# A two-layer encoder step on one core: TensorE kept in program order within the gate and up products, and the norm's roots placed between them

## The chip, the core and the metric

The kernel runs on one core of a Trainium2 chip. A core has TensorE for matrix products (PE in the profile; its weight loads are listed apart as PEld), VectorE (DVE), ScalarE (ACT), GpSimd (POOL) and SyncE (SP), which issues most transfers. Each takes its own queue of instructions in order and waits on semaphores for the others. The metric is the device time of one execution in microseconds; less is better.

## The reference

One step of a hybrid streaming encoder for 560 columns: 512 frames of a new stream, 32 frames of a running stream and 16 meta tokens, each a vector of 1024. Two layers; each is a feed-forward half-step, a mixer, and another feed-forward half-step. The first layer's mixer is a gated linear attention (GLA), the second's a latent attention (MLA).

```python
def rmsnorm(x, w):
    x32 = x.astype(jnp.float32)
    y = x32 * lax.rsqrt(jnp.mean(x32 * x32, axis=-1, keepdims=True) + RMS_EPS)
    return (y * w.astype(jnp.float32)).astype(x.dtype)

def swiglu_half(h, norm_w, w_gate, w_up, w_down):
    hn = rmsnorm(h, norm_w)
    return h + 0.5 * ((jax.nn.silu(hn @ w_gate) * (hn @ w_up)) @ w_down)

for i in range(DEPTH):
    hp = swiglu_half(hp, ffn1_norm[i], ffn1_w_gate[i], ffn1_w_up[i], ffn1_w_down[i])
    ...
    xp = rmsnorm(hp, mix_norm[i])
    ...                       # GLA for i = 0, MLA for i = 1; hp = hp + dp
    hp = swiglu_half(hp, ffn2_norm[i], ffn2_w_gate[i], ffn2_w_up[i], ffn2_w_down[i])
```

All data is float32. The inner size of the feed-forward part is 2816, that is 22 tiles of 128.

## The kernel before

**Layout.** Activations lie with the 1024 features on partitions, as 8 tiles of 128, and the columns beside each other. The state `h` stays on the chip. The columns are treated in two halves of 280 (272 in the last feed-forward part, which leaves the meta tokens out). Each float32 operand is split into a rounded high part and the rest: ScalarE casts the high part (`whi`, `ah`, `x`; L323), VectorE subtracts to get the low part (`wlo`, `al`, `x`; L324). A product is then high x high, low weight x high, high weight x low: lines 352, 353 and 355 in `mm`, where 352 and 353 alternate over the tiles of the sum, so that the second matmul of a product already needs `wlo`.

**Four feed-forward parts.** `ffn` goes over groups of the 22 inner tiles, and in a group over pairs of tiles. `gate_up` makes gate and up for a pair with seven products instead of eight, by a Strassen-like scheme over a 2 x 2 split of the input (4 feature tiles by half of the columns). The products are called by their operand and are written in this order: b11 into bank pair A, b21 into C, t6 added into A, t5 into B, t7 added into A, t4 into C, b22 added into B. Each is 24 matmuls. `quads` loads the four weight quarters (tile `fr`, L429), adds them on VectorE (L438), and hands out the split weights one product at a time; three of its additions stand ahead of the weight of t6. After a product, `copy` (L483) or `finish` (L489 to L499) takes results out on ScalarE and VectorE; `finish` multiplies by the norm's root `yn`, applies silu and splits the result into `ah` and `al`. Between two products `gap` lets `ffn` put in pieces of the product down of the group before (tile `Y`, bank pair of its own, result added into `h` on L544). The last group's down is written after all pairs of the part.

**The operands of a feed-forward part** are made while `h` gets its last additions, tile by tile: class `Quads` writes for each feature tile the split operand, the combinations t5, t6, t7, t4 of it, and the square of `h`, summed over tiles in `acc`. In the first part (`lazy`) there is no earlier product, so that each operand and the squares are made when first asked for.

**The norm's roots.** The operands carry the norm's weight but not the root of the mean square, which is one number per column; it is multiplied in at the end, by `finish`. `roots` makes it short: three matmuls with one column each sum `acc` over partitions and put 280 sums into three columns (L394, six instructions each time), VectorE does the root on a 128 x 3 tile (L408 to L416, eleven small operations one after the other), and the returned function transposes the three columns against the identity (L401), which gives the root in every partition; `scale` copies it to `yn` on ScalarE (L264). `rsqrt_mean` makes it long: one sum with all columns (L380), and the same root on a 128 x 280 tile with squares on ScalarE (L412). `scale` of class `Normed`, which the two mixers use, is long; `scale` of `Quads` is short, and makes sums, root and transposes at one place, the first `finish`.

**The order** of instructions on each engine is not the written order. The library plans it: it runs the program in a simulation and gives an engine the first written instruction among those that are ready there. So the written order is a priority, and what the simulation believes to be late falls behind.

Of the kernel before, what the change touches and what calls it, by code (L numbers as in the profile page):

```python
# [10 lines left out]
F32 = mybir.dt.float32  # L11
# [7 lines left out]
P = 128  # L19
D = 1024  # L20
ND = D // P
# [31 lines left out]
def weight_plan():  # L53
# [3 lines left out]
    def ffn(i, l):  # L57
        for gi, (f0, f1) in enumerate(GROUPS):
# [3 lines left out]
            for m in range(ND):  # L62
                plan.append((("d", i, l, gi, m), f1 - f0))

    ffn(1, 0)
    for h in range(GH):
        plan.extend((("v", h, j), nk * V_COLS[h] / P) for j, nk in enumerate(V_PARTS[h]))
# [4 lines left out]
        if h >= 2:  # L72
            plan.extend((("go", h - 2, c), 8) for c in range(4))
    ffn(2, 0)
    ffn(1, 1)
    for m in range(6):
        plan.append((("wd", m), 8))
# [18 lines left out]
class Normed(list):  # L96
# [3 lines left out]
    def __init__(self, net, name, halves):  # L100
        self.net, self.w0, self.halves, self.y = net, NORM_COLS[name], halves, None
        self.squared, self.scaled = [0, 0], [False, False]
# [22 lines left out]
    def scale(self, hf):  # L125
        c = slice(*self.halves[hf])
        if not self.scaled[hf]:
            while self.squared[hf] < ND:
                self.square(hf)
            self.net.rsqrt_mean(hf, self.y[:, c], c.stop - c.start, D)  # L130
            self.scaled[hf] = True
        return self.y[:, c]


class Quads(Normed):
# [10 lines left out]
    def __init__(self, net, name, halves, pool, tmp):  # L146
        super().__init__(net, name, halves)
        self.pool, self.tmp = pool, tmp
        self.n = halves[0][1]
        self.sets, self.kept, self.made = None, {}, set()  # L150
        self.lazy, self.early = False, []

    def place(self, op, i):

# [74 lines left out]
    def make(self, op):  # L229
# [24 lines left out]
                net.split(*self.place("b22", i), b22)  # L254
        self.made.add(op)

    def scale(self, hf):
        net = self.net
        c0, c1 = self.halves[hf]
        if not self.scaled[hf]:  # L260
            if self.lazy:
                for m in range(ND):
                    Normed.square(self, hf)
            net.nc.scalar.copy(self.y[:, c0:c1], net.roots(hf, c1 - c0, D)())  # L264
            self.scaled[hf] = True
        return self.y[:, c0:c1]

# [14 lines left out]
class Net:  # L282
# [90 lines left out]
            nc.scalar.activation(sq[:, :n], src, AF.Square)  # L373
            nc.vector.tensor_tensor(acc[:, :n], acc[:, :n], sq[:, :n], op=ALU.add)

    def rsqrt_mean(self, half, y, n, dim):

        nc = self.nc
        s = self.bank("s")
        nc.tensor.matmul(s[:, :n], self.ones, self.accs[half][:, :n], start=True, stop=True)  # L380
        vh = self.np_.tile([P, 280], F32, name="vh", tag="vh", bufs=1)
        t = self.np_.tile([P, 280], F32, name="t", tag="t", bufs=1)
        self.rsqrt(y, s[:, :n], vh[:, :n], t[:, :n], dim)

    def roots(self, half, n, dim):

        pe = self.nc.tensor
        acc = self.accs[half]  # L390
        s = self.bank("s")
        first = (0, P, n - P)
        for j, c in enumerate(first):
            pe.matmul(s[:, j:j + 1], acc[:, c:c + P], self.ones[:, :1], start=True, stop=True)  # L394
        y, vh, t = (self.np_.tile([P, 3], F32, name=x, tag=x) for x in ("ry", "rv", "rt"))
        self.rsqrt(y, s[:, :3], vh, t, dim)

        def finish():
            out = self.bank("s")
            for j in (2, 0, 1):  # L400
                pe.transpose(out[:, first[j]:first[j] + P], y[:, j:j + 1].to_broadcast([P, P]), self.ident)  # L401
            return out[:, :n]

        return finish
# [55 lines left out]
    def gate_up(self, i, l, f, xs, act, raws, tp, between):  # L460


        nc = self.nc
        v = nc.vector
        n = xs.n
        left = self.quads(i, l, f, raws, xs.early)
        done = []

        def product(to, op, more=False):
            if xs.lazy and op in ("b11", "b21"):  # L470
                w, x = next(left), xs.operand(op)
            else:
                x, w = xs.operand(op), next(left)
            for j in range(2):
                self.mm(to[:, j, :n], w, 4 * j, x, (0, n), more)

        def gap():
            done.append(0)
            between(len(done))

        def copy(of, tag):
            r = tp.tile([P, 2, 280], F32, name="r", tag=tag, bufs=1)
            nc.scalar.copy(r[:, :, :n], of[:, :, :n])  # L483
            return r

        def finish(j, hf, bank, r, how):
            gu = tp.tile([P, 2, 280], F32, name="gu", tag="gu", bufs=2)
            b, r, t = bank[:, :, :n], r[:, :, :n], gu[:, :, :n]
            if how == "neg":  # L489
                v.scalar_tensor_tensor(t, b, -1.0, r, op0=ALU.mult, op1=ALU.subtract)  # L490
            else:
                v.tensor_tensor(t, b, r, op=how)
            y = xs.scale(hf).unsqueeze(1).to_broadcast([P, 2, n])
            v.tensor_tensor(t, t, y, op=ALU.mult)
            g, u = gu[:, 0, :n], gu[:, 1, :n]
            nc.scalar.activation(g, g, AF.Silu)
            v.tensor_tensor(g, g, u, op=ALU.mult)
            c = slice(*xs.halves[hf])
            self.split(act[j][0][:, c], act[j][1][:, c], g)  # L499

        A = self.bank2("A")
        product(A, "b11")
        r1 = copy(A, "ra")
        gap()
        C = self.bank2("C")
        product(C, "b21")
        first = xs.lazy and "t6" not in xs.made
        if not first:
            finish(0, 0, C, r1, ALU.add)
        gap()  # L510
        product(A, "t6", True)
        r2 = copy(A, "rb")
        gap()
        B = self.bank2("B")
        product(B, "t5")
        p5 = copy(B, "rc")
        if first:
            finish(0, 0, C, r1, ALU.add)
        gap()
        product(A, "t7", True)  # L520
        r3 = copy(A, "ra")
        finish(1, 1, A, p5, "neg")
        gap()
        D = self.bank2("C")
        product(D, "t4")
        finish(1, 0, D, r3, ALU.subtract)
        gap()
        product(B, "b22", True)
        finish(0, 1, B, r2, ALU.add)
        gap()  # L530
# [19 lines left out]
    def ffn(self, i, l, xs, halves, side, turn):  # L550


        ap, fw = Pools(self.tc, side), Pools(self.tc, side)
        acp = ap(f"act{i}{l}")
        if xs.lazy:
            free = [acp.tile([P, 2, T // 2], F32, name="xt", tag=f"a{x}{j}") for j in range(4, 8) for x in "hl"]
            xs.tmp = [t[:, k, :] for t in free for k in range(2)]
        raws, tp = fw(f"raw{i}{l}", 6), fw(f"tmp{i}{l}", 1)
        fill = []
        last = len(GROUPS) - 1  # L560
        for gi, (f0, f1) in enumerate(GROUPS):
            j0 = 4 * (gi % 2) if gi < last else 0
            acts = [(acp.tile([P, T], F32R, name=f"ah{j}", tag=f"ah{j}"),
                     acp.tile([P, T], F32R, name=f"al{j}", tag=f"al{j}")) for j in range(j0, j0 + 4 if gi == last else j0 + f1 - f0)]
            slots = [7 * min((f1 - f0) // 2, 2) - 1]

            def between(k):
                if slots[0] <= 0 or (slots[0] == 7 * min((f1 - f0) // 2, 2) - 1 and k < 2):
                    return
                for _ in range(-(-len(fill) // slots[0])):  # L570
                    fill.pop(0)()
                slots[0] -= 1

            for f in range(f0, f1, 2):
                if gi == last and f == f0 + 4:
                    assert not fill
                    acts += [(acp.tile([P, T], F32R, name=f"ah{j}", tag=f"ah{j}"),
                              acp.tile([P, T], F32R, name=f"al{j}", tag=f"al{j}")) for j in range(4, 8)]
                self.gate_up(i, l, f, xs, acts[f - f0:f - f0 + 2], raws, tp, between)
            assert not fill  # L580
            order = [(m, hf) for m in range(ND) for hf in (0, 1)]
            if gi < last:
                fill = self.down(i, l, gi, acts, halves, order)
        fw.close()
        after = turn()
        order = Quads.ORDER if isinstance(after, Quads) else (
            [(0, 0), (1, 0), (0, 1), (1, 1), (2, 0), (3, 0), (2, 1), (3, 1)] + [(m, hf) for hf in (0, 1) for m in range(4, 8)])
        for f in self.down(i, l, last, acts, halves, order, after):
            f()
        ap.close()  # L590
# [966 lines left out]
```

## Time and profile before

| | us |
|---|---|
| median of 3 runs | 2114.17 |
| lowest, highest | 2113.81, 2117.72 |
| the profiled execution | 2115.19 |
| its span | 2113.4 |
| TensorE busy with matmuls | 2028.2 |
| VectorE busy | 1649.3 |
| ScalarE busy | 1021.5 |

In the span, the first feed-forward part runs from 0 to about 412 us, GLA to 675, the second part to 1072, the third to 1465, MLA to 1705 and the last part to the end. A row of a timeline has the start in us, the length in us, engine, line and operation, what is written and read with shapes, the count, and in brackets the idle time ahead of it with what ended it. In shares and windows, "x24" is a count of instructions. The granted clock is 1.00 at full speed of TensorE and 0.50 at half.

### The profile page before, as it was taken

How to read it: one execution, taken by the hardware profiler on the slowest of the kernel's cores; microseconds unless marked ns; L12 is line 12 of the kernel's file. 1: busy time of each engine (PE TensorE's matmuls, PEld its weight loads, DVE VectorE, ACT ScalarE, POOL GpSimd, SP SyncE). 2: the span in 40 equal slices, each digit the busy share in tenths (PEclk: the TensorE clock that was granted, in tenths of full speed). 3: DMA queues.
4: the chain of work that ended last, by engine and by line, in shares of the span. 5: the costliest groups of instructions: out<-in, count | busy, mean ns of one | idle time of the engine just before them, and what ended most of it. 6: DMA issues, size and time to landing. Idle time of an engine off the chain costs nothing.

```text
span 2113.4 us, 37954 instructions
## 1 busy us (share of the span) xinstructions
PE 2028.2 (96%) x15262; PEld 1981.8 (94%) x15262; DVE 1649.3 (78%) x3085; ACT 1021.5 (48%) x1830; POOL 52.0 (2%) x117
## 2 busy tenths in 40 slices
PE   5999999999998999999989999999999979999997
PEld 5999999989997899999979999999988969999997
DVE  7887878666658888788778877886887778877874
ACT  6444445455445444444545444454675445444441
POOL 0000000101110000000000000000210000000000
PEclk8999999999999999999999999999999979999998
DMA  4323232222221232322223323222112123333221
GB/s 130 103 88 107 93 96 78 77 73 73 66 83 58 89 102 80 105 80 91 76 80 95 106 90 96 90 83 92 60 52 68 46 88 97 96 101 99 87 72 62
DMA packets 91905, 180.16 MB, mean 85 GB/s; under 512 B 10240, under 2 KB 21888, under 8 KB 91728
## 3 DMA queue, kind: packets, MB, share of 16 engines
q1 hardware_dynamic: 87904, 173.09, 25.9%
q10 hardware_dynamic: 3824, 4.63, 0.7%
q8 instruction: 120, 1.97, 0.4%
q14 instruction: 57, 0.47, 0.1%
HBM read 173.69 MB, written 3.99 MB: 84 GB/s over the span
## 4 chain that ended last, share of the span: by engine, by line
PE 78%; DVE 14%; ACT 3%; issue 2%; DMA 2%; POOL 0%; SPq 0%; DVEq 0%; ACTq 0%; POOLq 0%
PE Y L355 8%; PE Y L352 8%; PE Y L353 8%; PE A L353 5%; PE A L355 5%; PE A L352 5%; DVE wlo L324 4%; PE ps L352 3%; PE B L353 3%; PE ps L355 3%; PE B L355 3%; PE ps L353 3%; PE B L352 3%; PE C L353 3%; PE C L355 3%; PE C L352 3%
## 5 line engine op out<-in xcount | busy, mean ns | idle before, releaser
L324 DVE TENSOR_TENSOR wlo<-fr,whi 128x1024 fp32r<-128x1024 f32 x308 | 372.2, 1218 | 15.1 <-ACT whi L323 13.7
L352 PE MATMUL Y<-ah,whi 128*128 128x280 f32 (+1 forms) x1408 | 374.8, 292 | 6.1 <-ACT ah L323 5.2
L353 PE MATMUL Y<-ah,wlo 128*128 128x280 f32 (+1 forms) x1408 | 374.2, 292 | 0.0
L323 ACT CAST whi<-fr 128x1024 fp32r<-128x1024 f32 x308 | 319.6, 1049 | 94.8 <-PE C L355 33.1
L352 PE MATMUL A<-x,whi 128*128 128x280 f32 (+1 forms) x1056 | 287.4, 297 | 15.5 <-ACT whi L323 15.2
L353 PE MATMUL A<-x,wlo 128*128 128x280 f32 (+1 forms) x1056 | 287.2, 297 | 6.0 <-DVE wlo L324 6.0
L352 PEld LDWEIGHTS Y<-ah,whi 128*128 128x128 f32 x1408 | 265.8, 189 | 8.0 <-ACT ah L323 6.7
L544 DVE SCALAR_TENSOR_TENSOR h<-Y,h 128x280 f32<-128x280 f32 (+1 forms) x320 | 141.3, 444 | 163.1 <-PE Y L355 162.5
L353 PEld LDWEIGHTS Y<-ah,wlo 128*128 128x128 f32 x1408 | 265.9, 189 | 0.0
L324 DVE TENSOR_TENSOR wlo<-raw,whi 128x512 fp32r<-128x512 f32 (+5 forms) x231 | 196.6, 853 | 74.8 <-ACT whi L323 74.5
L323 ACT CAST whi<-raw 128x512 fp32r<-128x512 f32 (+5 forms) x231 | 169.7, 736 | 169.5 <-PE ps L355 49.6
L438 DVE TENSOR_TENSOR fr<-fr 128x1024 f32<-128x1024 f32 x176 | 214.7, 1220 | 25.5 <-DMA fr<-W 23.6
L355 PE MATMUL Y<-al,whi 128*128 128x280 f32 (+1 forms) x1408 | 233.1, 291 | 0.0
L352 PEld LDWEIGHTS A<-x,whi 128*128 128x128 f32 x1056 | 204.5, 194 | 16.3 <-ACT whi L323 15.7
L353 PEld LDWEIGHTS A<-x,wlo 128*128 128x128 f32 x1056 | 204.3, 193 | 8.2 <-DVE wlo L324 8.2
L355 PEld LDWEIGHTS Y<-al,whi 128*128 128x128 f32 x1408 | 200.5, 189 | 0.0
L353 PE MATMUL C<-x,wlo 128*128 128x280 f32 (+1 forms) x704 | 188.5, 293 | 3.3 <-DVE wlo L324 3.3
L352 PE MATMUL B<-x,whi 128*128 128x280 f32 (+1 forms) x704 | 187.2, 291 | 2.3 <-ACT whi L323 2.3
L352 PE MATMUL C<-x,whi 128*128 128x280 f32 (+1 forms) x704 | 188.5, 292 | 0.0
L353 PE MATMUL B<-x,wlo 128*128 128x280 f32 (+1 forms) x704 | 186.4, 291 | 1.0 <-DVE wlo L324 1.0
L355 PE MATMUL A<-x,whi 128*128 128x280 f32 (+1 forms) x1056 | 181.8, 295 | 0.0
L483 ACT COPY r<-A 128x560 f32<-128x560 f32 (+1 forms) x132 | 82.2, 623 | 174.7 <-PE A L355 170.9
(374 smaller groups left out, 4071.1 us busy)
## 6 DMA issues: line engine op xcount, KB each, us to landing
fr<-W SPq DMA_DIRECT2D x352, 256.0 KB, 3.4
raw<-W SPq DMA_DIRECT2D x80, 512.0 KB, 3.5
raw<-W SPq DMA_DIRECT2D x100, 256.0 KB, 3.0
raw<-W SPq DMA_DIRECT2D x40, 128.0 KB, 2.1
h<-xT SPq DMA_DIRECT2D x3, 560.0 KB, 7.4
raw<-W SPq DMA_DIRECT2D x4, 384.0 KB, 3.0
o_y<-h SPq DMA_DIRECT2D x8, 136.0 KB, 1.8
o_y<-h ACTq DMA_DIRECT2D x8, 136.0 KB, 1.8
```

The lines of the kernel that those rows point to most:

```text
L323: self.nc.scalar.copy(hi, src)
L324: self.nc.vector.tensor_tensor(lo, src, hi.bitcast(F32), op=ALU.subtract)
L352: f(hi[:, b0 + k, :], xh[:, c], start=not more and k == 0, stop=False)
L353: f(lo[:, b0 + k, :], xh[:, c], start=False, stop=False)
L355: f(hi[:, b0 + k, :], xl[:, c], start=False, stop=k == n - 1)
L438: add = lambda out, x, y: nc.vector.tensor_tensor(out, x, y, op=ALU.add)
L483: nc.scalar.copy(r[:, :, :n], of[:, :, :n])
L544: nc.vector.scalar_tensor_tensor(self.h[:, m, c], Y[:, :n], 0.5, self.h[:, m, c], op0=ALU.mult, op1=ALU.add)
```

## The change

Three things. Each call of `gate_up` stands in a region in which the library must keep TensorE's instructions in the written order; the other engines, and the order of TensorE against the others, stay planned. The roots are written in two steps: `xs.roots(hf)` writes the sums and the small root operations, `scale` the transposes and the copy. In the first call of a part the sums of half 0 stand after b21 (after t6 in the lazy part), its transposes and the finishing of (0, 0) after t5, the sums of half 1 behind these, and its transposes after t7; in later calls nothing moves but what the region fixes. In the mixers the long roots are replaced with the short ones, sums and transposes at one place.

```diff
@@ Normed.scale
-            self.net.rsqrt_mean(hf, self.y[:, c], c.stop - c.start, D)
+            self.net.nc.scalar.copy(self.y[:, c], self.net.roots(hf, c.stop - c.start, D)())
@@ Quads
+    def roots(self, hf):
+
+        c0, c1 = self.halves[hf]
+        if self.lazy:
+            for m in range(ND):
+                Normed.square(self, hf)
+        self.finish[hf] = self.net.roots(hf, c1 - c0, D)
+
     def scale(self, hf):
-        net = self.net
         c0, c1 = self.halves[hf]
         if not self.scaled[hf]:
-            if self.lazy:
-                for m in range(ND):
-                    Normed.square(self, hf)
-            net.nc.scalar.copy(self.y[:, c0:c1], net.roots(hf, c1 - c0, D)())
+            self.net.nc.scalar.copy(self.y[:, c0:c1], self.finish[hf]())
             self.scaled[hf] = True
         return self.y[:, c0:c1]
@@ Net: rsqrt_mean is removed
@@ gate_up
+        first = not xs.finish
         A = self.bank2("A")
         product(A, "b11")
         r1 = copy(A, "ra")
         gap()
         C = self.bank2("C")
         product(C, "b21")
-        first = xs.lazy and "t6" not in xs.made
         if not first:
             finish(0, 0, C, r1, ALU.add)
         gap()
+        if first and not xs.lazy:
+            xs.roots(0)
         product(A, "t6", True)
         r2 = copy(A, "rb")
         gap()
+        if first and xs.lazy:
+            xs.roots(0)
         B = self.bank2("B")
         product(B, "t5")
         p5 = copy(B, "rc")
         if first:
             finish(0, 0, C, r1, ALU.add)
+            xs.roots(1)
         gap()
@@ ffn
-                self.gate_up(i, l, f, xs, acts[f - f0:f - f0 + 2], raws, tp, between)
+                with self.tc.manual_schedule(engines={mybir.EngineType.PE}):
+                    self.gate_up(i, l, f, xs, acts[f - f0:f - f0 + 2], raws, tp, between)
```

More of the change, by code (lines that the diff above doesn't have):

```diff
@@ L150, in __init__ @@
         self.sets, self.kept, self.made = None, {}, set()
-        self.lazy, self.early = False, []
+        self.lazy, self.early, self.finish = False, [], {}
     def place(self, op, i):
@@ L374, in square @@
             nc.vector.tensor_tensor(acc[:, :n], acc[:, :n], sq[:, :n], op=ALU.add)
[L376 to L383, printed above, removed]
     def roots(self, half, n, dim):
```

## The prediction

> **What bounds the kernel now.** I read the page's share of engines first, then the waits of TensorE alone, then windows cut at the places where TensorE stood still, then the timeline there. From the page, the busy share and the granted clock:
>
> ```profile
> PE 2028.2 (96%) x15262; PEld 1981.8 (94%) x15262; DVE 1649.3 (78%) x3085; ACT 1021.5 (48%) x1830; POOL 52.0 (2%) x117
> ...
> PEclk8999999999999999999999999999999979999998
> ```
>
> TensorE is the bound: 2113.4 - 2028.2 = 85 us without a matmul is all that better ordering can win, and the clock falls in few slices. What TensorE waited for (engine, tile, line, releaser: us, times, longest):
>
> ```profile
> PE Y L401 <- DVE ry L416: 21.0, 8, 3.3
> ...
> PE Y L394 <- DVE acc L222: 14.4, 3, 5.9
> PE A L353 <- DVE wlo L324: 6.0, 5, 2.9
> ```
>
> The first two rows, 35.4 us, are the norm's roots: L394 sums the squares over partitions and waits for their accumulation, L401 transposes the finished roots and waits for VectorE. Nearly all of it stands at the entry of the three feed-forward parts behind the first (675, 1071 and 1705 us), as the windows show (length, then busy us and instructions of PE, PEld, DVE, ACT, POOL, then granted clock, DMA share, GB/s):
>
> ```profile
> 675.00:690.50 15.50, 3.94 (x19) 3.75 (x19) 11.32 (x38) 5.38 (x9) 0.00 (x0) 0.66 0.52 170
> 690.50:698.40 7.90, 7.90 (x50) 7.61 (x49) 6.54 (x6) 3.15 (x5) 0.00 (x0) 0.80 0.00 0
> 698.40:715.86 17.46, 15.96 (x122) 15.55 (x121) 14.53 (x18) 9.14 (x13) 0.00 (x0) 1.00 0.36 122
> ...
> 1071.70:1083.40 11.70, 3.33 (x19) 3.14 (x19) 7.74 (x30) 3.55 (x5) 0.00 (x0) 0.68 0.00 0
> 1083.40:1091.20 7.80, 7.80 (x50) 7.39 (x48) 6.45 (x6) 3.05 (x5) 0.00 (x0) 0.82 0.00 0
> 1091.20:1108.60 17.40, 16.07 (x122) 15.63 (x121) 14.51 (x17) 9.21 (x13) 0.00 (x0) 1.00 0.40 121
> 1705.00:1720.40 15.40, 4.00 (x19) 3.78 (x19) 11.21 (x38) 5.40 (x9) 0.00 (x0) 0.58 0.33 98
> 1720.40:1728.50 8.10, 8.10 (x50) 7.81 (x49) 5.33 (x5) 3.36 (x5) 0.00 (x0) 0.75 0.36 137
> 1728.50:1749.85 21.35, 18.08 (x122) 17.65 (x121) 17.30 (x22) 10.97 (x16) 0.00 (x0) 0.84 0.30 100
> ```
>
> Three rows for each entry: the wait with 18 root matmuls in it; the products b11 and b21, 48 matmuls, partly at low clock; the five products t6 to b22, 120 matmuls. The scheduler had placed all 18 root matmuls ahead of b11, and TensorE takes its queue in order. So 15.5, 11.7 and 15.4 us pass in which the roots, not the weights, hold the engine. Why it costs so much is seen at the first entry:
>
> ```profile
> 680.65 1.12 ACT L323 CAST x<-q 128x1120 fp32r<-128x1120 f32 x1 [1.15 <-DVE q L205]
> ...
> 682.91 1.32 DVE L324 TENSOR_TENSOR x<-q,x 128x1120 fp32r<-128x1120 f32 x1
> ...
> 686.96 1.05 ACT L323 CAST whi<-fr 128x1024 fp32r<-128x1024 f32 x1
> ...
> 689.82 1.23 DVE L324 TENSOR_TENSOR wlo<-fr,whi 128x1024 fp32r<-128x1024 f32 x1
> ...
> 693.44 5.00 DVE L438 TENSOR_TENSOR fr<-fr 128x1024 f32<-128x1024 f32 x4
> ...
> 698.67 0.74 DVE L492 TENSOR_TENSOR gu<-C,r 128x560 f32<-128x560 f32 x1 [0.23 <-PE C L355]
> ```
>
> ScalarE is done with the last operand at 681.77 and casts the first weight only at 686.96, because the copy of the first half's roots stands ahead of it in its queue; VectorE makes wlo after both chains of root operations. b11 needs wlo at its second matmul.
>
> **The change part by part.** First, **the order in the three entries**. Program order inside a gate-and-up call is b11, b21, sums of half 0, t6, t5, transposes 0, sums 1, t7, transposes 1, t4, b22. The 18 matmuls stay; they move from ahead of b11 to between the products. Their cost there, by the distance from one start to the next in a stage at full clock, and the old long sum of the mixers beside it:
>
> ```profile
> 1465.32 0.63 PE L380 MATMUL s<-acc,ones 128*128 128x280 f32 x2
> 1465.58 0.50 PE L352 MATMUL s<-x,whi 128*128 128x280 f32 x1
> ...
> 1478.64 0.72 PE L394 MATMUL s<-ones,acc 128*128 128x1 f32 x6
> 1479.22 0.37 PE L352 MATMUL ps<-x,whi 128*128 128x280 f32 x1
> ...
> 1485.14 0.49 PE L401 MATMUL s<-ident,ry 128*128 128x128 f32 x3
> 1485.38 0.89 PE L355 MATMUL ps<-x,whi 128*128 128x280 f32 x5
> ```
>
> Sums of one half 0.58, transposes 0.24 to 0.3 (I take 0.27), old long sum 0.26 us. A first gate-and-up call thus carries 2 x 0.85 = 1.7 us of root work on TensorE's path, where nothing hides it; 0.58 of it lies ahead of t6, 1.12 behind.
>
> When can b11 start? Without roots ahead of them, ScalarE casts the weight and VectorE forms wlo right behind the last operand. First entry: cast of x ends 681.77; whi to 682.8; VectorE forms the operand's low part 681.8 to 683.1, then wlo 1.23: b11 at 684.3. From there 7.90 for b11 and b21 (the low clock kept as measured), 0.58, 15.96 for five products without their gaps, 1.12: end at 709.9 instead of 715.86, **6.0 us** won. The other two entries need these rows:
>
> ```profile
> 1074.15 1.12 ACT L323 CAST x<-q 128x1120 fp32r<-128x1120 f32 x1 [0.79 <-DVE q L205]
> ...
> 1082.72 1.22 DVE L324 TENSOR_TENSOR wlo<-fr,whi 128x1024 fp32r<-128x1024 f32 x1
> ...
> 1082.92 0.87 PE L401 MATMUL Y<-ident,ry 128*128 128x128 f32 x3 [2.31 <-DVE ry L416]
> ...
> 1710.55 1.10 ACT L323 CAST x<-q 128x1088 fp32r<-128x1088 f32 x1 [1.10 <-DVE q L205]
> ...
> 1712.82 1.28 DVE L324 TENSOR_TENSOR x<-q,x 128x1088 fp32r<-128x1088 f32 x1
> ...
> 1714.18 21.33 SPq L429 DMA_DIRECT2D fr<-W  x16
> ...
> 1717.77 1.04 ACT L323 CAST whi<-fr 128x1024 fp32r<-128x1024 f32 x1 [0.84 <-DMA fr<-W]
> ...
> 1728.78 0.72 DVE L492 TENSOR_TENSOR gu<-C,r 128x544 f32<-128x544 f32 x1 [1.73 <-PE C L355]
> ```
>
> Second entry: cast ends 1075.27, low part (1.32) 1076.6, wlo (1.22) 1077.8 = b11. Then 7.80 + 0.58 + 16.07 + 1.12 gives 1103.4 against 1108.60: **5.2 us**. Third entry: here SyncE's queue is passed too. Its weight transfers are issued at 1714.18, right behind the operand's low part, which stood behind a root operation that waited for TensorE. Free of it, the low part runs 1711.65 to 1712.95, the issue moves to about 1713.05 and the landing, 3.6 us after it as before, to 1716.65; whi 1717.7, wlo 1718.9 = b11. Then 8.10 + 0.58 + 15.5 (15.96 x 272/280 columns; the 18.08 measured holds a second fall of the clock, 0.84) + 1.12: 1744.2 against 1749.85: **5.6 us**. Together 16.8.
>
> What is late next. t6 needs three additions of weights (3.75 of the 5.00 us), a cast (1.05) and wlo (1.23). In the first entry these run 685.5 to 691.5, ahead of the 692.8 at which t6 could start. But the root operations of half 0 lie in VectorE's one queue near them, and the first waits for the sums. If wlo of t6 is queued behind some of them, t6 slips; the least is 0 and the most, with the whole 2.31 us chain and wlo ahead, 692.8 + 2.31 + 1.23 = 696.3, 3.5 late. I take 1.3, below the middle, since the chain leaves room between its steps. Transposes 1 need the chain of half 1 (2.31) behind t7 (3.1 us), with about 2 us of finishing work in the same queue: 0 to 1.5, I take 0.7. So 2.0 us a stage are lost again, 6.0 together: **10.8 us** remain (ends 16.8 and 1.8).
>
> **The first feed-forward part** gets the same order, but there VectorE is the bound while it builds operands one by one:
>
> ```profile
> 24.00:52.00 28.00, 21.41 (x115) 20.29 (x116) 24.89 (x68) 17.46 (x33) 0.00 (x0) 0.68 0.18 57
> ...
> 35.13 0.37 PE L352 MATMUL A<-x,whi 128*128 128x280 f32 x1
> ...
> 41.34 0.89 PE L394 MATMUL Y<-ones,acc 128*128 128x1 f32 x5 [0.33 <-DVE acc L374]
> ```
>
> VectorE idles 3.1 of 28 us, so no order gains more than that. On the other side the sums of half 1, which waited for their squares until 41.34, now stand ahead of t7, which began at 35.13; if the squares stay that late, t7 slips by 6.2 us. Nearest to the row, with VectorE's total unchanged, is **0** (ends +3.1 and -6.2).
>
> **The mixers.** Four long roots (one 0.26 us sum each) become four short ones (0.85 us): 4 x 0.59 = 2.4 us more TensorE work where TensorE is nearly always busy. VectorE and ScalarE lose wide operations (twelve squares among them) that stood beside matmuls; that hides already. In the stretch behind the first mixer's roots TensorE idles 38.00 - 34.84 us:
>
> ```profile
> 412.00:450.00 38.00, 34.84 (x249) 30.94 (x247) 24.29 (x42) 22.79 (x46) 5.86 (x11) 1.00 0.26 85
> ```
>
> An earlier root could at best remove those 3.2 us. I take a **loss of 2.0** (ends: loss 2.4, gain 0.8).
>
> Later gate-and-up calls already run in program order, one product and two down pieces at a time, and nothing is stored or loaded differently: 0. A wait that program order adds holds everything behind it on TensorE; those are the t6 and transposes waits priced above.
>
> Sum: 10.8 + 0 - 2.0 = 8.8 us. The profiled execution took 2115.19 (span 2113.4 and 1.8 around it), 1.0 above the median of 2114.17. 2115.19 - 8.8 - 1.0 = **2105 us**.
>
> [...] The rows agree that the clock is low after each wait (0.66, 0.68, 0.58, then 0.80, 0.82, 0.75). [...]
>
> **The rivals.** *Everything hides.* VectorE's order happens to suit: 16.8 from the entries, 3.1 in the first part, 0 lost in the mixers: 2115.19 - 19.9 - 1.0 = 2094. For it: the weights' work of t6 ends 1.3 us early when it runs as soon as it can. Against: one queue serves both.
>
> *The stall only moves.* t6 waits in each entry as long as now in the third, 2.9 us (the row of A behind wlo), transposes 0.7, and the clock falls again, worth 18.08 - 15.5 = 2.6 us: 5.6 - 6.2 = -0.6 a stage, -1.8 for three, mixers -2.0: 2118, within the measurement's grain. For it: the third entry shows just this. Against: there VectorE waited 1.73 us for C (the row at 1728.78) with wlo of t6 queued behind, and that finishing work is moved behind t5. [...]
>
> *Slower: the additions behind the roots.* Place: VectorE's queue between b21 and t6. If the three additions stand behind the root chain, then in the first entry sums end 692.8, chain 695.1, additions 698.8, cast 699.9, wlo 701.1 = t6, 8.3 us late: 6.0 - 8.3 - 0.7 = -3.0 a stage, three times 9, mixers 2: 2125. It decides from a slip of t6 of about 5 us on. Against: at 693.44 all four additions ran ahead of gu, which was ready as soon as b21 ended; the roots become ready later than that.
>
> **How the numbers follow.** Forecast 0.58 (2100 to 2110), all hidden 0.17, moved stall 0.16, slower 0.09. A difference under 0.2% (4.2 us) can hardly be told from none here. Faster by more than that means under 2109.9: forecast and all hidden, with a little of either edge, 0.76; same 0.15; slower 0.09. The range 2094 to 2114 leaves out the slower case, half of the moved stall and a little below.
>
> **What would show it.** In the new trace L394 and L401 stand between products, never ahead of b11 in the three entries; b11 begins near 684, 1077 and 1718 less what was won before; the 14.4 us row of sums waiting for squares vanishes. A wait of A for wlo at t6 tells the stall's size. The prediction is wrong if that wait exceeds 5 us, if the first part loses over 5 us, or if the mixers lose more than 3.

## The result

| | before | after |
|---|---|---|
| median, us | 2114.64 (7 runs) | 2121.74 (7 runs) |
| lowest, highest, us | 2113.4, 2117.72 | 2120.28, 2130.06 |
| ratio to before, 95% interval | | 1.0037 [1.0023, 1.0052] |

The change costs 7.1 us; 2105 was forecast. The profiled execution of after has a span of 2119.7 us, 6.3 more than the one of before. In after the lines have moved: casts L327, low parts L328, matmuls L356, L357 and L359, additions of weights L432; the sums are L388, the transposes L395, the small root operations L402 to L410, `finish` L484 to L491.

First the page of after: TensorE's row and its granted clock over 40 slices.

```profile
PE 2031.8 (96%) x15290; PEld 1985.5 (94%) x15290; DVE 1642.9 (78%) x3097; ACT 1018.4 (48%) x1822; POOL 51.4 (2%) x117
...
PEclk8999999999999999999999999999999989999999
```

TensorE is busy 3.6 us longer with the same products, and idle 2.7 us longer (87.9 against 85.2). The waits of TensorE in after (us, times, longest):

```profile
PE A L356 <- ACT whi L327: 41.6, 6, 12.8
PE Y L395 <- DVE ry L410: 12.8, 8, 3.8
PE A L357 <- DVE wlo L328: 9.3, 9, 1.8
PE A L356 <- DVE gu L484: 5.5, 3, 2.5
PE Y L388 <- DVE acc L378: 3.1, 2, 1.5
```

The row of 14.4 us of sums waiting for squares is gone, as forecast, and the transposes wait 12.8 us where they waited 21.0. In their place the first weight cast is waited for, 41.6 us (15.2 in before), and a new row is there: a product into bank A that waits for `finish` (L484) to have read that bank.

Everything that follows goes by one measure: from the last matmul before a later feed-forward part to the first matmul of its first down product. Between these stand the same 216 matmuls of nine products and the roots, in any order: the first call of `gate_up` and b11 and b21 of the next. The windows of before, summed over the three entries, then those of after one by one and summed (length, busy us and instructions of PE, PEld, DVE, ACT, POOL; then granted clock, DMA share, GB/s):

```profile
sum 140.91, PE 103.47 PEld 100.79 DVE 113.04 ACT 62.80 POOL 0.00; mean PE 34.49 PEld 33.60 DVE 37.68 ACT 20.93 POOL 0.00
```

```profile
679.78:728.38 48.60, 34.81 (x235) 33.61 (x235) 39.86 (x72) 21.18 (x34) 0.00 (x0) 0.86 0.35 111
1076.71:1123.12 46.41, 35.84 (x235) 34.64 (x235) 36.16 (x64) 19.25 (x30) 0.00 (x0) 0.85 0.19 60
1712.39:1765.41 53.02, 35.45 (x235) 34.50 (x235) 39.53 (x72) 22.37 (x35) 0.00 (x0) 0.81 0.32 102
sum 148.03, PE 106.10 PEld 102.75 DVE 115.55 ACT 62.80 POOL 0.00; mean PE 35.37 PEld 34.25 DVE 38.52 ACT 20.93 POOL 0.00
```

The entries grew from 140.9 to 148.0, by 7.1 us, where they were forecast to shrink by 10.8. That is as much as the medians differ, but the rest of the kernel did not stand still in these two profiles: after is 4.7 us late before the first entry, and makes up 5.6 us between the entries and behind the last, which nothing here explains. What stands in the entries, in windows of after:

```profile
679.78:689.06 9.28, 0.60 (x2) 0.29 (x2) 8.39 (x16) 5.74 (x9) 0.00 (x0) 0.68 0.77 245
...
1076.71:1082.78 6.07, 0.60 (x1) 0.29 (x1) 4.92 (x9) 4.11 (x5) 0.00 (x0) 0.69 0.00 0
...
1712.39:1726.44 14.05, 0.60 (x2) 0.29 (x1) 8.32 (x16) 5.01 (x8) 0.00 (x0) 0.68 0.32 95
...
696.76:700.17 3.41, 2.26 (x19) 2.05 (x18) 2.25 (x4) 1.89 (x3) 0.00 (x0) 1.00 0.00 0
700.17:703.58 3.41, 3.41 (x17) 3.41 (x16) 3.41 (x8) 0.00 (x0) 0.00 (x0) 0.50 0.91 278
...
710.41:713.82 3.41, 1.92 (x16) 1.70 (x15) 2.74 (x8) 2.33 (x4) 0.00 (x0) 1.00 0.01 2
```

The first three rows end at b11's second matmul, the first that needs `wlo`: it starts 9.28, 6.07 and 14.05 us after the last matmul before the part (forecast 9.3, 6.05, 13.8). The next two rows show what is new: after a stretch of 3.41 us with 2.26 us of matmuls in it, the clock is at 0.50 for the next 3.41 us. Such a fall comes once behind b11 and b21 at the first entry and twice at each of the others (from 1092.70, 1113.18, 1737.83 and 1751.48 on, each 3.41 us at 0.50). Busy time alone does not decide it: the last row has only 1.92 us of matmuls, and the clock stayed at 1.00 behind it. TensorE at the first entry, where it waited behind b21:

```profile
697.16 0.72 PE L388 MATMUL Y<-ones,acc 128*128 128x1 f32 x6
...
699.27 0.40 PE L357 MATMUL A<-x,wlo 128*128 128x280 f32 x1 [1.15 <-DVE wlo L328]
...
707.41 0.54 PE L395 MATMUL Y<-ident,ry 128*128 128x128 f32 x3 [0.30 <-DVE ry L410]
707.78 0.73 PE L388 MATMUL Y<-ones,acc 128*128 128x1 f32 x6
...
713.18 0.39 PE L356 MATMUL A<-x,whi 128*128 128x280 f32 x1 [1.49 <-DVE gu L484]
...
718.70 0.54 PE L395 MATMUL Y<-ident,ry 128*128 128x128 f32 x3 [2.18 <-DVE ry L410]
```

t6 waits 1.15 us for `wlo`, transposes 0 for 0.30. Then comes something that is not in the written order: the matmul at 713.18 is b11 of the *next* pair. The region holds the order within one call of `gate_up`; between calls the library may choose, and it put that product ahead of transposes 1. It waits 1.49 us for bank A, and the transposes wait 2.18 us all the same. The second entry looks the same (1.49 and 2.16); at the third the early b11 waits 2.49 and the transposes no more. Why they are late is seen in VectorE's queue. The first two rows belong to half 0 and t6; from 708.55 on it is half 1, from its first root operation (`rv`) to its last (`ry`):

```profile
697.92 0.16 DVE L402 TENSOR_SCALAR rv<-Y 128x3 f32<-128x3 f32 x1 [1.97 <-PE Y L388]
698.00 1.22 DVE L328 TENSOR_TENSOR wlo<-fr,whi 128x1024 fp32r<-128x1024 f32 x1
...
708.55 0.16 DVE L402 TENSOR_SCALAR rv<-Y 128x3 f32<-128x3 f32 x1
708.66 1.23 DVE L432 TENSOR_TENSOR fr<-fr 128x1024 f32<-128x1024 f32 x1
709.80 0.73 DVE L488 TENSOR_TENSOR gu<-gu,yn 128x560 f32<-128x560 f32 x1
710.45 0.16 DVE L403 TENSOR_SCALAR ry<-rv 128x3 int32<-128x3 int32 x1
710.52 1.22 DVE L328 TENSOR_TENSOR wlo<-fr,whi 128x1024 fp32r<-128x1024 f32 x1
711.66 0.44 DVE L491 TENSOR_TENSOR gu<-gu 128x280 f32<-128x280 f32 x1
712.02 0.15 DVE L408 TENSOR_TENSOR rt<-ry 128x3 f32<-128x3 f32 x1
...
716.43 0.16 DVE L409 TENSOR_TENSOR rt<-rt,rv 128x3 f32<-128x3 f32 x1
716.55 1.22 DVE L432 TENSOR_TENSOR fr<-fr 128x1024 f32<-128x1024 f32 x1
717.69 0.15 DVE L410 SCALAR_TENSOR_TENSOR ry<-rt,ry 128x3 f32<-128x3 f32 x1
...
718.49 0.16 DVE L410 SCALAR_TENSOR_TENSOR ry<-rt,ry 128x3 f32<-128x3 f32 x1
```

Eleven links of 0.16 us take 10.1 us, because VectorE has other work ready by now: ten operations of 0.4 to 1.2 us stand between the links. Ahead of b11, where before had them, the same chains ran almost alone, in 3.2 and 2.1 us. The first and last link of half 1 in before, at the second entry, which is like the first:

```profile
1080.65 0.16 DVE L408 TENSOR_SCALAR rv<-Y 128x3 f32<-128x3 f32 x1 [2.06 <-PE Y L394]
...
1082.61 0.16 DVE L416 SCALAR_TENSOR_TENSOR ry<-rt,ry 128x3 f32<-128x3 f32 x1
```

And `wlo` of t6 stands in after behind an `rv` that waits 1.97 us for its sums.

### The profile page after: what moved, and what is told of

Same layout as the page of the kernel before. It is cut to its first block, busy times and chain, and to the rows that moved or that the text cites. A ratio compares the mean times of both kernels' runs of the same rounds, so it can differ in the third digit from the quotient of the medians.

```text
span 2119.7 us, 38004 instructions
## 1 busy us (share of the span) xinstructions
PE 2031.8 (96%) x15290; PEld 1985.5 (94%) x15290; DVE 1642.9 (78%) x3097; ACT 1018.4 (48%) x1822; POOL 51.4 (2%) x117
## 3 DMA queue, kind: packets, MB, share of 16 engines
q8 instruction: 120, 1.97, 0.4%
## 4 chain that ended last, share of the span: by engine, by line
PE 80%; DVE 12%; ACT 3%; DMA 2%; issue 2%; POOL 0%; SPq 0%; DVEq 0%; ACTq 0%; POOLq 0%
PE Y L359 8%; PE Y L356 8%; PE Y L357 8%; PE A L357 6%; PE A L359 5%; PE A L356 5%; DVE wlo L328 4%; PE ps L356 3%; PE C L357 3%; PE C L359 3%; PE C L356 3%; PE B L357 3%; PE B L359 3%; PE B L356 3%; PE ps L359 3%; PE ps L357 3%
## 5 line engine op out<-in xcount | busy, mean ns | idle before, releaser
L328 DVE TENSOR_TENSOR wlo<-fr,whi 128x1024 fp32r<-128x1024 f32 x308 | 372.3, 1218 | 18.3 <-ACT whi L327 17.1
L356 PE MATMUL Y<-ah,whi 128*128 128x280 f32 (+1 forms) x1408 | 373.2, 291 | 2.2 <-ACT ah L327 1.5
L357 PE MATMUL Y<-ah,wlo 128*128 128x280 f32 (+1 forms) x1408 | 372.8, 291 | 0.0
L327 ACT CAST whi<-fr 128x1024 fp32r<-128x1024 f32 x308 | 319.7, 1049 | 94.2 <-PE C L359 36.9
L356 PE MATMUL A<-x,whi 128*128 128x280 f32 (+1 forms) x1056 | 291.7, 300 | 47.1 <-ACT whi L327 41.6
L357 PE MATMUL A<-x,wlo 128*128 128x280 f32 (+1 forms) x1056 | 290.7, 300 | 9.4 <-DVE wlo L328 9.3
L356 PEld LDWEIGHTS Y<-ah,whi 128*128 128x128 f32 x1408 | 264.9, 188 | 3.4 <-ACT ah L327 2.1
L357 PEld LDWEIGHTS Y<-ah,wlo 128*128 128x128 f32 x1408 | 265.0, 188 | 0.0
L328 DVE TENSOR_TENSOR wlo<-raw,whi 128x512 fp32r<-128x512 f32 (+5 forms) x231 | 196.6, 853 | 78.4 <-ACT whi L327 73.7
L327 ACT CAST whi<-raw 128x512 fp32r<-128x512 f32 (+5 forms) x231 | 169.8, 736 | 178.4 <-PE ps L359 53.9
L356 PEld LDWEIGHTS A<-x,whi 128*128 128x128 f32 x1056 | 207.4, 196 | 48.8 <-ACT whi L327 42.7
L359 PE MATMUL Y<-al,whi 128*128 128x280 f32 (+1 forms) x1408 | 233.4, 291 | 0.0
L432 DVE TENSOR_TENSOR fr<-fr 128x1024 f32<-128x1024 f32 x176 | 214.8, 1221 | 18.3 <-DMA fr<-W 16.1
L357 PEld LDWEIGHTS A<-x,wlo 128*128 128x128 f32 x1056 | 207.4, 196 | 12.2 <-DVE wlo L328 12.1
L359 PEld LDWEIGHTS Y<-al,whi 128*128 128x128 f32 x1408 | 200.3, 188 | 0.4
L356 PE MATMUL B<-x,whi 128*128 128x280 f32 (+1 forms) x704 | 187.2, 291 | 1.0 <-ACT whi L327 1.0
L356 PE MATMUL C<-x,whi 128*128 128x280 f32 (+1 forms) x704 | 188.1, 292 | 0.0
L357 PE MATMUL B<-x,wlo 128*128 128x280 f32 (+1 forms) x704 | 187.1, 291 | 1.0 <-DVE wlo L328 0.9
L357 PE MATMUL C<-x,wlo 128*128 128x280 f32 (+1 forms) x704 | 187.8, 293 | 0.0
L359 PE MATMUL A<-x,whi 128*128 128x280 f32 (+1 forms) x1056 | 183.8, 297 | 0.0
```

What stands on the lines that cost most here:

```text
L327: self.nc.scalar.copy(hi, src)
L328: self.nc.vector.tensor_tensor(lo, src, hi.bitcast(F32), op=ALU.subtract)
L356: f(hi[:, b0 + k, :], xh[:, c], start=not more and k == 0, stop=False)
L357: f(lo[:, b0 + k, :], xh[:, c], start=False, stop=False)
L359: f(hi[:, b0 + k, :], xl[:, c], start=False, stop=k == n - 1)
L432: add = lambda out, x, y: nc.vector.tensor_tensor(out, x, y, op=ALU.add)
```

## The experiments

The theory after this comparison: the sums and the chain of roots must run where VectorE is free; only one product ahead of their transposes, in a full queue, they come late, and TensorE in program order waits. The rivals: the mixers' short roots cost the time; the region itself does; the early b11 does; the lazy first part does. Each kernel stands against runs of before on the same chip ("entries" is the sum of the three windows in its profile, 140.9 in before):

| kernel | median us | before us | ratio, 95% | entries us |
|---|---|---|---|---|
| mixers only | 2115.71 | 2116.13 | 0.9996 [0.9986, 1.0006] | 141.0 |
| order only (no mixers) | 2123.49 | 2116.13 | 1.0033 [1.0020, 1.0046] | 146.7 |
| region only | 2139.22 | 2116.13 | 1.0106 [1.0093, 1.0119] | 162.3 |
| split only (no region) | 2110.61 | 2116.13 | 0.9969 [0.9957, 0.9982] | 138.4 |
| both sums before t6 | 2109.87 | 2114.68 | 0.9975 [0.9965, 0.9985] | 135.1 |
| chain doubled | 2145.02 | 2114.68 | 1.0142 [1.0128, 1.0156] | 161.7 |
| chain shortened | 2115.41 | 2114.68 | 1.0004 [0.9996, 1.0013] | 144.9 |
| both sums before b11 | 2104.21 | 2114.68 | 0.9952 [0.9939, 0.9964] | 130.2 |
| one region over a part | 2131.36 | 2115.31 | 1.0078 [1.0065, 1.0091] | 161.4 |
| chain on GpSimd | 2130.07 | 2115.31 | 1.0073 [1.0061, 1.0085] | 154.9 |
| first part left free | 2108.29 | 2115.31 | 0.9966 [0.9954, 0.9978] | 132.1 |
| one chain for both halves | 2101.08 | 2115.31 | 0.9943 [0.9930, 0.9956] | 133.1 |

Against before, the entries change as the span of the same profile does, within 5 us, except with the chain doubled (7.5). Six of the twelve medians lie outside every range expected of them, by 0.6 to 7 us: order only, split only, both sums before t6, both kernels with another length of chain, and the one with the first part left free.

**Which part of the change.** Mixers only is before with the new line in `Normed.scale`; order only is after with the old one; region only is before with the region around `gate_up`; split only is order only without the region.

```diff
 # mixers only, against before
-            self.net.rsqrt_mean(hf, self.y[:, c], c.stop - c.start, D)
+            self.net.nc.scalar.copy(self.y[:, c], self.net.roots(hf, c.stop - c.start, D)())
 # region only, against before
-                self.gate_up(i, l, f, xs, acts[f - f0:f - f0 + 2], raws, tp, between)
+                with self.tc.manual_schedule(engines={mybir.EngineType.PE}):
+                    self.gate_up(i, l, f, xs, acts[f - f0:f - f0 + 2], raws, tp, between)
```

> The kernel before with short roots in the two mixers and nothing else. If the mixers pay for the added matmuls of the short roots (4 x 0.59 us of work, measured shifts of 1.2 and 1.9 us at the two mixer entries of the changed kernel), it takes 2116 to 2118 us, 1 to 3 above the kernel before. If the whole loss of the change lies in the feed-forward parts, it takes the kernel before's 2114.6 within 1 us.

> The changed kernel with the long roots put back in the mixers: program order and split roots in the feed-forward parts alone. If mixers and feed-forward parts add up, it takes 2118 to 2120 us (2121.7 less 2 to 3). If the mixers are harmless, 2121 to 2122.

> The kernel before with TensorE in program order in the gate-and-up calls, and the roots left in one piece: sums and transposes of half 0 both between b21 and t6. If what costs is the root chain drawn out in VectorE's queue (about 10 us in the changed kernel), TensorE now waits for the whole of it twice at every entry, 6 to 9 us more at each of three entries than in the changed kernel: 2130 to 2145 us. If it is program order as such (a stall at any place alike), it takes about the order-only kernel's 2118 to 2122.

> The order-only kernel without the region: roots written in two steps and between the products, but TensorE's order left to the planner. If the written place is only a priority, the planner puts sums and transposes ahead of b11 again as in the kernel before, and it takes 2112 to 2116 us, with L394's and L401's counterparts ahead of b11 at the three entries. If the split alone moves the roots, it takes about the order-only kernel's time, 2118 to 2120, or, with transposes free to wait their turn, less than 2110.

The mixers show no effect: the interval of their ratio reaches from -3.0 to +1.3 us. The loss is in the order. Program order with the roots in one piece is the worst of these four; its waits of TensorE:

```profile
PE Y L401 <- DVE ry L416: 30.7, 9, 6.4
```

Here TensorE stands through whole chains. Writing the sums ahead of the transposes, the second part of the change, therefore gains some 15 us (1.0106 to 1.0033) on what the region costs. Without the region the library puts sums and transposes ahead of b11 again, and the kernel is 0.3% faster than before. Why it is faster stays open: its entries are 2.5 us shorter, its span 7.3.

**How far the sums must stand ahead.** In order only, the sums of half 1 move from behind t5 to the place of those of half 0, between b21 and t6; in the other kernel both go ahead of b11, with the transposes left where they are:

```diff
 # both sums before t6, against order only
         if first and not xs.lazy:
             xs.roots(0)
+            xs.roots(1)
         product(A, "t6", True)
...
-            xs.roots(1)
+            if xs.lazy:
+                xs.roots(1)
 # both sums before b11: the same, but these lines stand ahead of product(A, "b11")
+        if first and not xs.lazy:
+            xs.roots(0)
+            xs.roots(1)
```

> The order-only kernel with the sums of half 1 written beside those of half 0, between b21 and t6, in the three later parts. If TensorE's waits ahead of transposes 1 come from the chain of half 1 being drawn out in VectorE's queue behind t5 (10.1 us for 2.1 us of work), that chain now ends under t7 and the two waits there (1.5 and 2.2 us and a low-clock stretch after them) go, 3 to 4 us an entry: about 2112 to 2114 us where the order-only kernel has 2123.5. If program order costs elsewhere, 2122 to 2125.

> The order-only kernel with the sums of both halves written ahead of b11 in the three later parts, the transposes where the change has them. The sums then run while TensorE waits for the first weight, and the chains run in VectorE's queue while little else is ready there. By the drawn-out chain the waits at t6 and at both transposes go (1.2, 0.3, 1.5 and 2.2 us an entry, and the low clock after them), and b11 comes 1 to 3 us later, behind the chains: 2106 to 2112. If the chains hold the first weight as long as the whole wait saved, 2118 to 2122.

Both are faster than before. The windows of the second, summed, and VectorE in it at the first entry (its root operations are L411 to L419):

```profile
sum 130.16, PE 99.44 PEld 97.92 DVE 109.28 ACT 62.48 POOL 0.00; mean PE 33.15 PEld 32.64 DVE 36.43 ACT 20.83 POOL 0.00
```

```profile
688.36 0.16 DVE L411 TENSOR_SCALAR rv<-Y 128x3 f32<-128x3 f32 x1 [1.18 <-PE Y L397]
...
689.64 0.16 DVE L411 TENSOR_SCALAR rv<-Y 128x3 f32<-128x3 f32 x1 [0.92 <-PE Y L397]
...
691.15 0.15 DVE L418 TENSOR_TENSOR rt<-rt,rv 128x3 f32<-128x3 f32 x1
691.22 0.15 DVE L417 TENSOR_TENSOR rt<-ry 128x3 f32<-128x3 f32 x1
...
692.78 0.16 DVE L419 SCALAR_TENSOR_TENSOR ry<-rt,ry 128x3 f32<-128x3 f32 x1
692.89 2.36 DVE L328 TENSOR_TENSOR wlo<-fr,whi 128x1024 fp32r<-128x1024 f32 x2
```

VectorE has idled and is waiting for the sums; both chains are done 4.6 us after the first `rv`, one long operation between them, and b11's second matmul waits 4.12 us for `wlo` behind them. Then nothing waits any more at this entry (at the third t6 still waits 0.93 us). That matmul comes later than in after, 13.19 us behind the last one before the part in place of 9.28, and yet the entries are 17.9 us shorter. Against before, of the roots only the transposes and the copy on ScalarE have moved, not the sums.

**The length of the chain.** The loop of `rsqrt` runs 6 times, or once, where the tile has three columns (once leaves two refinements of the root out, so that kernel stands for its time alone):

```diff
-        for _ in range(3):
+        for _ in range(self.steps if y.shape[-1] == 3 else 3):     # steps = 6, or 1, in the feed-forward parts
```

> The order-only kernel with six root iterations instead of three in the four feed-forward parts: 9 more links of about 0.19 us in each chain. If a chain is drawn out by one long operation of VectorE between two links (some 0.85 us a link), each of the chains gets 7 to 8 us longer and TensorE waits for it: 40 to 55 us more, 2160 to 2180. If a link costs only itself, 8 x 9 x 0.19 = 14 us at the most: up to 2138.

> The order-only kernel with one root iteration instead of three in the four feed-forward parts; two refinements of the root are left out. Five links instead of eleven: by the drawn-out chain both transposes find their root ready, and 2.2 + 1.5 + 0.3 us and the low-clock stretch go at each of three entries, about 4 in the first part: 2104 to 2110. If the waits have another cause, 2120 to 2123 (6 links x 0.19 us off each chain).

Both directions move the time as the theory says, but by less: nine links more in each of eight chains cost some 23 us against order only (1.0142 to 1.0033), six fewer won 6. Both medians lie between the range of the theory and that of its rival. In the short one the transposes of the entries have ceased to wait, and yet it is no faster than before; its waits of TensorE:

```profile
PE A L359 <- DVE rt L421: 4.7, 2, 2.3
PE A L359 <- DVE gu L496: 4.0, 1, 4.0
```

These 8.7 us are, by their tile and place, again the next pair's b11, waiting for `finish` to have read bank A (2.34, 2.34 and 3.97 us at the three entries). So the chain was not the only thing in the way.

**The early b11.** One region over the whole part, in order only, forbids it; it also fixes the order of whole calls.

```diff
+        with self.tc.manual_schedule(engines={mybir.EngineType.PE}):
             for gi, (f0, f1) in enumerate(GROUPS):
...
                 for f in range(f0, f1, 2):
-                with self.tc.manual_schedule(engines={mybir.EngineType.PE}):
                     self.gate_up(i, l, f, xs, acts[f - f0:f - f0 + 2], raws, tp, between)
```

> The change without its short mixer roots, with TensorE's program order held over a whole feed-forward part and not per call: the next pair's b11 can no longer be placed ahead of transposes 1. Theory A (the early b11 only fills a wait that transposes 1 have anyway): transposes 1 and all behind them wait 3 to 5 us an entry with nothing between, 2124 to 2134. Theory B (the early b11, which waits 1.5 us for the finishing work that reads bank A, is itself the loss): the transposes wait about as long as now, the wait for A is gone, 2116 to 2121. The order-only kernel stood at 2123.5.

```profile
PE Y L404 <- DVE ry L419: 28.4, 9, 6.9
```

Without the early b11 transposes 1 wait 6.89, 6.89 and 6.22 us at the entries, with nothing between. It was a filler, not the cause: by placing it the library saved some 9 us (1.0078 to 1.0033), as far as the order of whole calls, which changed with it, costs nothing.

**The chain on another engine.** In order only, the loop of `rsqrt` goes to GpSimd for the three later parts, its last operation as two:

```diff
+        if self.on_pool:
+            v = self.nc.gpsimd
         for _ in range(3):
...
+            if self.on_pool:
+                v.tensor_scalar(t, t, 1.5, None, op0=ALU.add)
+                v.tensor_tensor(y, t, y, op=ALU.mult)
+            else:
                 v.scalar_tensor_tensor(y, t, 1.5, y, op0=ALU.add, op1=ALU.mult)
```

> The change without its short mixer roots, with all links of the root chains but the first two moved to GpSimd in the three later parts (12 operations there, as its one-operation link is split in two). GpSimd is idle then; from its 52.0 us for 117 operations an estimate of 0.45 us a link, 5.3 us a chain. Theory (the chain is slow because each link queues behind long operations in VectorE's queue): half 1's transposes are ready about 4 us earlier an entry, their 2.2 us wait and the 1.5 us wait for bank A go, 2110 to 2116 against 2123.5 of the order-only kernel. Rival (the loss lies in the wait for t6's weight and the fall of the clock there): these stay, 2119 to 2124. Second rival (a link on GpSimd takes over 0.8 us, so the chain stays near 10 us): 2121 to 2130.

The expectation of the theory missed by 14 us. The time is at the edge of the second rival's range, but that rival's condition, a chain of near 10 us, is not met. GpSimd at the first entry, half 1, with one operation of VectorE:

```profile
711.61 1.10 POOL L422 TENSOR_TENSOR rt<-ry 128x3 f32<-128x3 f32 x1 [5.41 <-DVE ry L415]
712.79 0.19 POOL L423 TENSOR_TENSOR rt<-rt,rv 128x3 f32<-128x3 f32 x1
...
714.02 1.22 DVE L331 TENSOR_TENSOR wlo<-fr,whi 128x1024 fp32r<-128x1024 f32 x1
714.17 1.12 POOL L423 TENSOR_TENSOR rt<-rt,rv 128x3 f32<-128x3 f32 x1
...
716.82 0.19 POOL L426 TENSOR_TENSOR ry<-rt,ry 128x3 f32<-128x3 f32 x1
```

With no other work on the engine the twelve operations take 5.4 us, and the two links left on VectorE took 2.0 us ahead of them: 7.4 in place of 10.1. t7, which is to cover this, lasts 3.1. Nor are the links rid of VectorE: 5 of the 24 at the first entry take 1.06 to 1.12 us, and each of these begins inside a 1.2 us operation of VectorE on 128 x 1024 and ends some 0.05 us behind it, as in the rows above; none of the other 19 begins inside one. The transposes still wait 5.1, 5.1 and 6.0 us, 3.8 us less in all than with the one region, and here too no b11 was placed ahead; the times of these two kernels cannot be told apart (1.0073 and 1.0078). So leaving VectorE's queue does shorten the chain, as the theory says, but distance is needed and not only an emptier queue. That the library, with another plan, dropped its filler was not foreseen.

**The first part, and one chain.** In the kernel with both sums ahead of b11, the region is left out in the lazy part; then, on top, one chain over six columns takes the place of two chains over three.

```diff
-                with self.tc.manual_schedule(engines={mybir.EngineType.PE}):
+                with ExitStack() as es:
+                    if not xs.lazy:
+                        es.enter_context(self.tc.manual_schedule(engines={mybir.EngineType.PE}))
 # one chain
-            xs.roots(0)
-            xs.roots(1)
+            xs.both_roots()      # 12 sums into 6 columns, one rsqrt on 128 x 6
```

> The kernel with the sums of both halves ahead of b11 in the later parts (2104.2 before), and the first feed-forward part left to the scheduler, as in the kernel before. Theory: program order costs the first part about 3 us (its transposes 1 wait 3.8 us for a chain between operand work), so 2099 to 2103. Rival: the first part's loss is made up by what follows it, as the shift of the later stages in single profiles suggests: 2103 to 2106.

> The kernel of the run with the first part left to the scheduler, and one chain of root operations over six columns for both halves in place of two chains of three: 11 small VectorE operations fewer at each of the three entries, all ahead of the low part of the first weight. Theory (a chain costs its number of links in VectorE's queue, not their width): b11's second matmul waits 2 us less an entry, 4 to 7 us in all below its neighbour: 2094 to 2099. Rival (what sets b11 is the weight's landing and cast, or strangers fill the freed slots): no difference, 2099 to 2103.

Leaving the first part to the library wins nothing: its 3.8 us wait for the transposes is gone, and a matmul into C waits 3.5 us for `wlo` instead. The one chain, VectorE at the first entry, and b11's second matmul:

```profile
689.03 0.17 DVE L433 TENSOR_SCALAR rv<-Y 128x6 f32<-128x6 f32 x1 [2.45 <-PE Y L418]
...
692.14 0.17 DVE L441 SCALAR_TENSOR_TENSOR ry<-rt,ry 128x6 f32<-128x6 f32 x1
692.25 2.36 DVE L331 TENSOR_TENSOR wlo<-fr,whi 128x1024 fp32r<-128x1024 f32 x2
...
693.53 0.60 PE L360 MATMUL A<-x,wlo 128*128 128x280 f32 x1 [4.09 <-DVE wlo L331]
```

b11's second matmul comes 13.17 us after the last matmul before the part, against 13.19 with two chains: no gain there. The single chain starts 1.3 us later behind the last matmul (8.67 against 7.38), since it needs all twelve sums, and each link waits 0.20 us for the one before; two chains of three columns fill each other's waits, and both kernels are done with the roots 11.95 us after that matmul. So the expected mechanism is refuted. What the rival forecast for b11, no difference, came true, but not through landing and cast: the weight's casts were done at 688.99, 3.3 us ahead of `wlo`. The median is the lowest of all, 7.2 us under its neighbour, as much as the theory had asked; the entries (133.1 against 132.1) do not show where, so that is not credited to it. The intervals of this kernel, of the one with both sums before b11 and of the one with the first part left free overlap pairwise; which of them is best is not settled. That they beat both kernels is. Nor is it settled that the region is needed: the interval of split only, which has none, overlaps with that of both sums before b11 (0.9957 against 0.9964).

## Why the prediction was wrong

- **b11 earlier: right.** 9.28, 6.07 and 14.05 us were measured against 9.3, 6.05 and 13.8, the SyncE queue's share at the third entry included.
- **t6 late by 1.3: right.** It waited 1.15 us at each entry, for the reason given: `wlo` stood in VectorE's queue behind the first root operation, which waited for the sums.
- **Transposes 1 late by 0.7: the step that failed.** I priced the chain of half 1 at its length ahead of b11, 2.31 us, and some 2 us of finishing work with it, behind 3.1 us of t7. It took 10.1 us. Nor did I see that the region ends with the call, so that a product of the next pair may come first. At the first entry the early b11 waited 1.49 and the transposes 2.18 us more, so 3.67 in place of 0.7, and over the three entries 9.8 in place of 2.1. Transposes 0, priced at nothing, waited 1.1 in all. The whole idle time behind b11 is 14.3 us (41.9 idle in the windows of after, less 27.6 ahead of b11), against the 6.0 that I allowed. That is 8.3 of the 17.9 us between forecast and measurement. The prediction had the row that speaks of this, VectorE 14.53 us busy out of 17.46 in just that stretch, and did not use it.
- **Full clock behind b11 and b21: the other half.** I took b11 and b21 with their slow share and everything behind them at full speed, 10 us at half clock in all (twice the length of those rows times what the clock lacks to 1). For b11 and b21 that was right: from b11's second matmul on they took 8.1, 7.6 and 8.0 us against 7.9, 7.8 and 8.1. But in after there are 29 us at half clock behind b11's second matmul (48 in the entries, 19 of it ahead of b11, worked out the same way), 19 more than I took; 17 of the 19 are the five falls behind b21. At 0.50 a matmul of 280 columns started 0.23 us after the one before it (701.27, 701.50), at 1.00 0.13 (703.86, 703.99), so the 19 us cost some 8 us of matmul time, an estimate from these starts. In the stretch ahead of the first fall, the one at 696.76, 0.72 of the 2.26 us busy were six matmuls of one column. Before has as much in its entries, 49, but 31 of it ahead of b11, where TensorE mostly waits. The rival in which the stall only moves had such a fall in it, priced at 2.6 us a stage after a wait of 2.9 us at t6; its mechanism is what came, at another place (transposes 1 more than t6), and its 2118 is 3.7 us too low.
- **The first part at 0:** open. In single profiles one of its down products, at 130 us in after, starts 3.0 us later than in before, and before the first entry after is 4.7 us late; whether the 5.6 us made up later belong to this is not known. With that part left to the library it starts 4.2 later, so the region is not what delays it.
- **The mixers at -2.0:** they measured 0.4 us faster, with 0 inside the interval. That the 2.4 us more of TensorE work found room in idle time, such as the 3.2 us of that stretch, is argued and was not traced.
- **Additions behind the roots** (the slower rival): refuted; the four additions ran at 690.95, ahead of the chain, as argued. The sign came out as in that rival, by another way, and that its 2125 is the nearest of the four numbers (3.3 us too high) is luck. Of my three conditions for being wrong (t6 over 5 us late, the first part over 5, the mixers over 3) none was met: the list lacked transposes 1.

## What to carry to other kernels

A chain of small dependent operations is stretched by what stands ready in the engine's queue at that moment, here from 2.1 to 10.1 us: price it from the busy share of the stretch that it moves to, not from its length where it ran before. When a wait blocks an engine that must keep program order, move apart the two ends, producer and consumer: here leaving the sums early, where VectorE idled, and moving only the transposes was worth some 17 us against moving both (0.9952 to 1.0033). And price a short wait on TensorE with the fall of the clock where the traces show one behind it: here 3.41 us at 0.50 behind a wait of 1.15 us, some 1.5 us of matmul time by an estimate from starts 0.23 us apart in place of 0.13.

## What was not expected of the hardware

Short waits were followed by half clock: in after a wait of 1.15 us with a few one-column matmuls in the same stretch, at each of the three entries (at the first the granted clock was 1.00 up to 700.17 and 0.50 for the 3.41 us behind). What decides is not shown: the stretch from 710.41 had less matmul time and no such fall. A link on an otherwise unused GpSimd mostly took 0.19 to 0.23 us, but at the first entry 1.06 to 1.12 us for the same operation on the same shape in the five cases in which it began inside a 1.2 us operation of VectorE on 128 x 1024. And a dependent link on VectorE followed the one before it by 0.20 us at 0.17 us of its own, while links of two interleaved chains followed each other by 0.07 to 0.12.
